# The mixer's elementwise work on GpSimd moved to VectorE and ScalarE

## The chip, the core and the metric

The kernel runs on one core of a Trainium2 chip. A core has a matrix engine (TensorE; PE in the profile, with its weight loads as PEld), VectorE (DVE), ScalarE (ACT) and GpSimd (POOL), which run side by side and wait for each other through semaphores, and queues that issue transfers between the device's memory and the on-chip memory; most of them are issued by SyncE (SP). The metric is the device time of one execution in microseconds (us), lower is better.

## The reference

One layer of a decoder, on 256 tokens of width 1024, in float32:

```python
mod = (silu(c) @ W_ada + b_ada)              # six rows of 1024: shift, scale, gate, twice
h   = rmsnorm(x) * (1 + scale1) + shift1
proj = h @ w_in                              # 1024 x 9224
y_a = stick_breaking_attention(q, k, v)      # 16 heads of 64
qk  = silu(causal_conv(proj_qk, conv_w, conv_b))   # four taps
y_b = rmsnorm(mlstm(qk, v, i, f)) * sigmoid(o)     # 4 heads of 256
x += gate1 * ((sigmoid(g_a) * (y_a @ W_a) + sigmoid(g_b) * (y_b @ W_b)) @ W_out)
h  = rmsnorm(x) * (1 + scale2) + shift2
x += gate2 * moe(h)                          # top 4 of 32 experts, clamped SwiGLU, 1024 wide
out = rmsnorm(x)
```

All up to `x += gate1 * ...` is the mixer. The experts' weights are some 400 MB, and they are read once.

## The kernel before

**Two parts.** The mixer stands first, then the experts. The experts' part multiplies the weights of one pair of experts after the other as they arrive, through a ring of slots of 1 MB each; its loads stand in order on SyncE's queue, and each waits until its slot has been read out. The last loads of the mixer and the first of the experts share these slots.

**High and low parts.** In the mixer each matrix product is taken as three products of rounded numbers: ScalarE copies a block `x` into a rounded form (the high part, `whi`, `yahi`, `ybhi`, `hhi`), and the low part is `x` minus the high part (`wlo`, `yalo`, `yblo`, `hlo`), by one `tensor_tensor` that reads two tiles on chip and writes a third. TensorE then multiplies high by high, high by low and low by high.

**The first stage** runs over eight slices `kt` of the width. `start_h(kt)` loads two rows of `W_ada`, makes the slice's scale and shift (`ada`, L169: two instructions on VectorE, each over 1024 columns of two on-chip operands, with a sum at the end), normalises the slice (L344, L346, L347), lets ScalarE round it to `hhi` (L348) and takes `hlo` (L349). `start_w(kt)` loads a slice of seven blocks of `w_in`, and in two pieces of 1024 and 768 columns ScalarE makes the high part (L332) and GpSimd the low part (L333). `start_c(kt)` issues 45 matmuls with these (L360, L363). The two buffers of high and low parts alternate between slices. L320 is the low part of the small weight of the gates.

**The attention and the mLSTM** take the other blocks of `w_in` through `chunk` (in four pieces of 512 columns: L220 the high part, L223 the low part). For the blocks named `shared` the low parts of the last two pieces stand on GpSimd, 24 in all. `conv` makes the four taps (L563, L565), ScalarE the sigmoid (L567), and GpSimd their product (L569), which the scores of the next head read. `split_b1` makes three bfloat16 parts of the experts' first bias on GpSimd (L466, L468, L469); it is used by the experts alone.

**Order.** Each engine works through its own list in order. A planner builds the lists from priorities and modelled costs; `tc.issue_after(x)` holds instructions back in the plan until `x` has been planned. `lows` collects the low parts on GpSimd, and the bias loads and some memsets on GpSimd are planned behind the last of them.

Of the kernel before, what the change touches and what calls it, by code (L numbers as in the profile page):

```python
# [18 lines left out]
AF = mybir.ActivationFunctionType  # L19
OP = mybir.AluOpType  # L20
# [43 lines left out]
def body(tc, a, out):  # L64
    nc = tc.nc
    mm = nc.tensor.matmul
    act = nc.scalar.activation
    tt = nc.vector.tensor_tensor
    ts = nc.vector.tensor_scalar
    stt = nc.vector.scalar_tensor_tensor  # L70
    f32 = lambda t: t.bitcast(F32)
# [15 lines left out]
    def next_slot(shape):  # L87

        p = slots.pop(0)
        slots.append(p)  # L90
        return p.tile(shape, F32, name=SLOT_NAME.get(p, "w"))

    def load(src, shape):
        w = next_slot(shape)
        nc.sync.dma_start(w, src)
        return w
# [59 lines left out]
    for n in range(2):  # L156
        pz = ps_z.tile([128, 2, 512], F32, name="pz")[:, 0]
        b = slice(512 * n, 512 * n + 512)
        with tc.issue_after(up):
            up = mm(pz, ones, crow[n], start=True, stop=True).ins  # L160
        s = spl.tile([128, 512], F32, name="whi")
# [44 lines left out]
        last = act(r, r, AF.Exp, scale=-0.5)  # L206
        return r, last.ins

    def chunk(src, shared=False, after=None):

        w = load(src, [128, KT, 256])
        out = []
        for qd in range(4):
            x = w[:, 2 * qd:2 * qd + 2, :]
            hi = spl.tile([128, 2, 256], F32R, name="whi")
            if after is not None and qd > 1:
                with tc.issue_after(after):
                    act(hi, x, AF.Copy)
            else:
                act(hi, x, AF.Copy)  # L220
            lo = spl.tile([128, 2, 256], F32R, name="wlo")
            eng = nc.gpsimd if shared and qd > 1 else nc.vector
            last = eng.tensor_tensor(lo, x, f32(hi), OP.subtract)  # L223
            if eng is nc.gpsimd:
                lows.append(last.ins)
            out.append((hi, lo))
        return out

    todo = []
    for c in range(2, 4):  # L230
        todo += [(a["w_in"][g], g > 3) for g in (c, 4 + c, 8 + c)[c == 2:]]
    for hd in range(4):
        todo += [(a["w_in"][g], g > 19) for g in (12 + hd, 16 + hd, 20 + hd, 24 + hd)]
    for c in range(4):
        todo += [(w, False) for w in (a["w_in"][28 + c], a["w_a"][c], a["w_in"][32 + c], a["w_b"][c])]
    todo += [(a["w_out"][c], False) for c in range(4)]
    ready = []

    def fetch(after=None):

        if todo:
            ready.append(chunk(*todo.pop(0), after))

    def take():
        if not ready:
            fetch()
        return ready.pop(0)

    def proj_T(w, mv, blocks=2):

        mhi, mlo = mv
        ps = ps_pj.tile([128, 2, T], F32, name="pj")
        for qd, (whi, wlo) in enumerate(w):
            for n in range(blocks):
                s = slice(128 * n, 128 * n + 128)
                for j in range(2):
                    kt = 2 * qd + j
                    last = kt == KT - 1
                    mm(ps[:, n, :], whi[:, j, s], mhi[:, kt, :], start=kt + n == 0, stop=False, skip_group_check=True)  # L259
                    mm(ps[:, n, :], whi[:, j, s], mlo[:, kt, :], start=False, stop=False, skip_group_check=True)  # L260
                    mm(ps[:, n, :], wlo[:, j, s], mhi[:, kt, :], start=False, stop=last, skip_group_check=True)  # L261
        return ps
# [46 lines left out]
    pif = ps_m.tile([128, 512], F32, name="pm")  # L309
    first.append(ps_m.tile([128, 512], F32, name="pm").rearrange("p (n t) -> p n t", n=2))  # L310
    wf, parts = {}, {}
    order, his, lows = [], [], []
    wi = mx.tile([128, KT, 64], F32, name="cv")
    nc.gpsimd.memset(wi, 0.0)
    nc.gpsimd.tensor_copy(wi[:, :, 0:4], wif[:, :, 0:4])
# [1 line left out]
    wihi, wilo = (mx.tile([128, KT, 64], F32R, name="cs") for _ in range(2))  # L317
    with tc.issue_after(rs1_ins):
        act(wihi, wi, AF.Copy)
    nc.gpsimd.tensor_tensor(wilo, wi, f32(wihi), OP.subtract)  # L320

    def start_w(kt):
        w = wf[kt] = next_slot([128, 1792])
        if kt:
            nc.sync.dma_start(w, a["w_first"][kt])
        else:
            for b in (slice(0, 1024), slice(1024, 1792)):
                nc.sync.dma_start(w[:, b], a["w_first"][kt][:, b])
        hi, lo = ((yahi, yalo), (ybhi, yblo))[kt % 2]
        for b in (slice(0, 1024), slice(1024, 1792)):  # L330
            x, h, l = (t[:, b] for t in (w, hi.rearrange("p a b -> p (a b)"), lo.rearrange("p a b -> p (a b)")))
            act(h, x, AF.Copy)  # L332
            lows.append(nc.gpsimd.tensor_tensor(l, x, f32(h), OP.subtract).ins)  # L333
        parts[kt] = hi, lo

    def start_h(kt):
# [28 lines left out]
    for kt in range(KT):  # L365
        if kt == KT - 1:
            start_w(kt)
            start_h(kt)
        else:
            start_h(kt)  # L370
            start_w(kt)
        start_c(kt)
# [66 lines left out]


    kp = ab.tile([128, 2, 2, T], F32, name="kp")
    with tc.issue_after(lows[-1]):
        nc.gpsimd.memset(kp[64:128, :, 0, :], 0.0)
        nc.gpsimd.memset(kp[0:64, :, 1, :], 0.0)

    qs, vs = {}, {}
    for c in range(2):
# [11 lines left out]
    def load_b1(g):  # L459
        bts[g] = mx.tile([128, 512], F32, name="bt", bufs=1)  # L460
        for i in range(4):
            nc.gpsimd.dma_start(bts[g][32 * i:32 * i + 32], a["b1"][:, 512 * g:512 * g + 512])

    def split_b1(g):
        bt, b = bts[g], b1s[:, 512 * g:512 * g + 512]
        nc.gpsimd.tensor_copy(b, bt)  # L466
        for lo in (64, 96):
            nc.gpsimd.tensor_tensor(bt[lo:128], bt[lo:128], b[lo:128], OP.subtract)  # L468
            nc.gpsimd.tensor_copy(b[lo:128], bt[lo:128])  # L469

    def step_of_b1(g):
        with tc.issue_after(lows[-1]):
            if g:
                split_b1(g - 1)
            if g < 4:
                load_b1(g)

    for c in range(4):
        if c > 2:
            qs[c] = mx.tile([128, 2, T], F32, name="q")  # L480
            pq = proj_T(take(), hT)
            fetch()
            act(qs[c], pq, AF.Copy, scale=0.125)
        q = qs[c]
        if c > 1:
            pk = proj_T(take(), hT)
            fetch()
        else:
            pk = first[1 + 4 * c]
# [10 lines left out]
        for n in range(2):  # L500
# [11 lines left out]
            l = mx.tile([128, 768], F32, name="l")  # L512
# [5 lines left out]
            hi = mx.tile([128, 768], F32R, name="so", bufs=1)  # L518
            lo = mx.tile([128, 768], F32R, name="sp")
# [3 lines left out]
            for x in (hi, lo):  # L523
                last = x is lo
# [18 lines left out]


    xpads = [ab.tile([128, 2, T + 4], F32, name=f"xpad{i}") for i in range(2)]
    with tc.issue_after(lows[-1]):
        for xp in xpads:
            nc.gpsimd.memset(xp[:, :, 0:3], 0.0)
    ve = ab.tile([128, 2, 260], F32, name="vext")
    with tc.issue_after(lows[-1]):  # L550
        nc.gpsimd.memset(ve[:, :, 256:260], 1.0)

    def conv(g, name):

        ps = proj_T(take(), hT)
        fetch()
        xp = xpads[g // 4]
        act(xp[:, :, 3:3 + T], ps, AF.Copy)
        y = mx.tile([128, 2, T], F32, name="cv")
        for n in range(2):  # L560
            ch = 2 * g + n
            tap_w = lambda j: col[:, C_CW + 4 * ch + j:C_CW + 4 * ch + j + 1]
            ts(y[:, n, :], xp[:, n, 0:T], tap_w(0), col[:, C_CB + ch:C_CB + ch + 1], op0=OP.mult, op1=OP.add)  # L563
            for j in range(1, 4):
                stt(y[:, n, :], xp[:, n, j:j + T], tap_w(j), y[:, n, :], OP.mult, OP.add)  # L565
        s = mx.tile([128, 2, T], F32, name="cs")
        act(s, y, AF.Sigmoid)  # L567
        r = mx.tile([128, 2, T], F32, name=name)
        nc.gpsimd.tensor_tensor(r, y, s, OP.mult)  # L569
        return r  # L570

    def qk_of(hd):
# [68 lines left out]
    last = None  # L641
    for hd in range(4):
# [6 lines left out]
        last = hd, read_out(hd, S), so  # L649
# [15 lines left out]
    for c in range(4):  # L665
        acc = []
        for mv in ((yahi, yalo), (ybhi, yblo)):
# [5 lines left out]
            s = mx.tile([128, 2, T], F32, name="sgate")  # L673
# [5 lines left out]
        y = acc[1]  # L679
# [26 lines left out]
    for c in range(4):  # L706
        w = take()
# [7 lines left out]
        for n in range(2):  # L715
            kt = 2 * c + n
            stt(xT[:, kt, :], po[n], mod_of(G1, kt), xT[:, kt, :], OP.mult, OP.add)
            x = xa[c // 2][:, kt % 4, :]
# [3 lines left out]
            for t in range(2):  # L722
                b = slice(128 * t, 128 * t + 128)
                mm(pl[:, 32 * t:32 * t + 32], x[:, b], rw[:, kt, :], start=False, stop=kt == KT - 1,
                   skip_group_check=True)
            for t in range(2):
                b = slice(128 * t, 128 * t + 128)
# [52 lines left out]
    def slots_of(p):  # L780

        G = wk.tile([128, 2, 2 * CAP], F32, name="G")
        for t in range(2):
            last = tt(G[:, t].rearrange("p (e s) -> p e s", e=2),
                      rank[:, t, 2 * p:2 * p + 2, None].to_broadcast([128, 2, CAP]),
                      iota[:, None, 0:CAP].to_broadcast([128, 2, CAP]), OP.is_equal)
        XG[p] = xgp.tile([128, KT, 2 * CAP], F32, name="xg")
        return G, last.ins

    XG, SS, ROWS = {}, {}, {}  # L790
    G0, last = slots_of(0)
# [299 lines left out]
    for n, (lo, width, step) in enumerate(LAST):  # L1091
        per = D // width
        for c in range(0, KT, per):
            w = next_slot([128, per, 2, width])
# [63 lines left out]
    for g in (3, 0, 1, 2):  # L1158
        b = xo[:, 2 * g:2 * g + 2, :]
        eng = nc.gpsimd if g == 3 else nc.vector  # L1160
        eng.tensor_tensor(b, b, rf[:, None, :].to_broadcast([128, 2, T]), OP.mult)  # L1161
    for g in (0, 1, 3, 2):
        eng = (nc.sync, nc.scalar)[g % 2]
# [63 lines left out]
```

## Time and profile before

| | us |
|---|---|
| median of 3 runs (lowest, highest) | 1349.43 (1348.67, 1350.36) |
| time of the profiled execution | 1350.39 |
| its span, first to last instruction | 1348.3 |
| VectorE busy | 485.9 |
| GpSimd busy | 151.3 |

The span is 2.1 us shorter than the time of the same execution. Busy time is the sum of the durations that the profiler shows, and an instruction that is held up while it runs counts as busy. The mixer takes about the first 400 us of the span.

### The profile page before, as it was taken

The numbers are of one execution on the slowest core, as the hardware profiler recorded it, in microseconds if no ns is written. First come the engines' busy times: TensorE is split into PE (matmuls) and PEld (weight loads), VectorE is DVE, ScalarE is ACT, GpSimd is POOL, SyncE is SP. The second block draws the span as 40 slices with busy tenths as digits, with TensorE's granted clock in tenths as the row PEclk, the third lists the DMA queues.
The fourth block names the chain that finished last, engine by engine and source line by source line (L and its number), as shares of the span: only waits on it lengthen the run. The fifth ranks groups of instructions, "written<-read, shape, count | busy, mean of one in ns | idle before, by whom it ended". The sixth has DMA issues, their size and how long they took to land. (4 is left out here: it accounts for less than half of the span.)

```text
span 1348.3 us, 16908 instructions
## 1 busy us (share of the span) xinstructions
PE 1239.2 (92%) x6859; PEld 675.8 (50%) x6874; DVE 485.9 (36%) x866; ACT 317.4 (24%) x600; POOL 151.3 (11%) x132
## 2 busy tenths in 40 slices
PE   7789989999998999999999999988999998899787
PEld 5777888999983443334433343332333333233323
DVE  6988888786550221121211212202121211201203
ACT  3256755655540210101101011010101101010102
POOL 5653455400000000000000000000000000000002
PEclk9899999999999999998999999999999999999989
DMA  9486465477579899999999999999999999999994
GB/s 361 150 302 226 167 255 183 168 313 283 218 278 420 364 410 421 419 419 420 421 419 420 420 420 420 421 419 420 420 421 420 419 421 420 419 420 420 419 419 163
DMA packets 70337, 483.46 MB, mean 359 GB/s; under 512 B 8134, under 2 KB 9558, under 8 KB 13676
## 3 DMA queue, kind: packets, MB, share of 16 engines
q1 hardware_dynamic: 69084, 480.54, 87.7%
q0 software_dynamic: 624, 1.23, 0.4%
q8 instruction: 57, 0.93, 0.3%
q10 hardware_dynamic: 544, 0.52, 0.1%
q14 instruction: 28, 0.23, 0.0%
HBM read 481.21 MB, written 1.05 MB: 358 GB/s over the span
## 5 line engine op out<-in xcount | busy, mean ns | idle before, releaser
L815 PE MATMUL s<-w,xg 128*64 128x512 f32 x1928 | 449.4, 602 | 29.9 <-DMA w<-in_w 26.6
L815 PEld LDWEIGHTS s<-w,xg 128*64 128x64 f32 x1928 | 125.5, 137 | 294.7 <-issue 206.8
L815 PE MATMUL t<-w,whi 128*64 128x512 f32 x908 | 204.2, 596 | 13.4 <-ACT whi L866 9.6
L832 DVE SCALAR_TENSOR_TENSOR xT<-pm,modT,xT 128x256 f32<-128x256 f32 x128 | 56.0, 479 | 392.9 <-PE pm L815 392.9
L815 PEld LDWEIGHTS t<-w,whi 128*64 128x64 f32 x908 | 61.7, 137 | 133.9 <-issue 103.7
L220 ACT ACTIVATE whi<-w 128x512 fp32r<-128x512 f32 x162 | 100.6, 630 | 85.1 <-PE pj L260 61.7
L850 ACT ACTIVATE wlo<-wlo 128x512 f32<-128x512 f32 x32 | 20.1, 630 | 424.7 <-DVE wlo L848 424.7
L223 DVE TENSOR_TENSOR wlo<-w,whi 128x512 fp32r<-128x512 f32 x140 | 101.2, 733 | 48.4 <-ACT whi L220 48.1
L261 PE MATMUL pj<-hhi,wlo 128*128 128x256 f32 x368 | 106.3, 289 | 8.8 <-DVE wlo L223 8.8
L848 DVE TENSOR_SCALAR wlo<-s 128x512 f32<-128x512 f32 x32 | 22.1, 692 | 246.2 <-PE s L815 225.1
L259 PE MATMUL pj<-hhi,whi 128*128 128x256 f32 x368 | 106.0, 288 | 0.0
L260 PE MATMUL pj<-hlo,whi 128*128 128x256 f32 x368 | 105.3, 286 | 0.0
L169 DVE CUSTOM_DVE_ANT_0 w<-w,silr,col 128x1024 f32<-128x1024 f32 x48 | 90.0, 1895 | 3.6 <-DMA w<-in_ada 3.4
L924 POOL CAST sel<-cst 128x128 bf16<-128x128 f32 x16 | 4.7, 296 | 746.2 <-PE s L815 746.2
L261 PEld LDWEIGHTS pj<-hhi,wlo 128*128 128x128 f32 x368 | 71.7, 195 | 10.2 <-DVE wlo L223 9.8
L259 PEld LDWEIGHTS pj<-hhi,whi 128*128 128x128 f32 x368 | 71.8, 195 | 0.5 <-issue 0.2
L260 PEld LDWEIGHTS pj<-hlo,whi 128*128 128x128 f32 x368 | 71.7, 195 | 0.1
L815 PEld LDWEIGHTS pm<-G,mghi 128*128 128x128 f32 x512 | 59.0, 192 | 17.6 <-issue 17.0
L815 PE MATMUL pm<-S,whi 128*128 128x256 f32 x240 | 67.3, 404 | 0.2 <-DVE xT L832 0.2
L815 PEld LDWEIGHTS pm<-S,whi 128*128 128x128 f32 x240 | 40.8, 189 | 50.0 <-issue 38.7
L815 PE MATMUL pm<-G,mghi 128*128 128x128 f32 x512 | 63.3, 279 | 0.2 <-ACT xg L843 0.2
L866 ACT ACTIVATE whi<-pm 128x512 f32<-128x512 f32 x32 | 19.1, 598 | 166.4 <-PE pm L818 166.4
(370 smaller groups left out, 1485.1 us busy)
## 6 DMA issues: line engine op xcount, KB each, us to landing
w<-in_w SPq DMA_DIRECT2D x354, 1024.0 KB, 19.9
w<-in_w_in SPq DMA_DIRECT2D x29, 1024.0 KB, 6.4
w<-in_ada SPq DMA_DIRECT2D x22, 1024.0 KB, 6.5
mglo<-in_w SPq DMA_DIRECT2D x19, 1024.0 KB, 19.9
w<-in_w_first SPq DMA_DIRECT2D x7, 896.0 KB, 14.4
w<-in_w_last SPq DMA_DIRECT2D x5, 1024.0 KB, 19.8
w<-in_w_a SPq DMA_DIRECT2D x4, 1024.0 KB, 7.0
w<-in_w_b SPq DMA_DIRECT2D x4, 1024.0 KB, 12.5
```

Source lines behind the costliest of these rows:

```text
L169: nc.vector.tensor_tensor_reduce(out=w[:, j + n, :], in0=w[:, j + n, :], in1=SILU[-1], scale=1.0, scalar=col[:, C_AB + i:C_AB + i + 1], op ...
L220: act(hi, x, AF.Copy)
L223: last = eng.tensor_tensor(lo, x, f32(hi), OP.subtract)
L259: mm(ps[:, n, :], whi[:, j, s], mhi[:, kt, :], start=kt + n == 0, stop=False, skip_group_check=True)
L260: mm(ps[:, n, :], whi[:, j, s], mlo[:, kt, :], start=False, stop=False, skip_group_check=True)
L261: mm(ps[:, n, :], wlo[:, j, s], mhi[:, kt, :], start=False, stop=last, skip_group_check=True)
L815: return tc.keep_in_program_order(mm(*args, **kw))
L832: stt(xT[:, kt, :], p[:, j, :], mod_of(G2, kt), xT[:, kt, :], OP.mult, OP.add)
L848: ts(g, glu, LIMIT, None, op0=OP.min)
L850: act(s, g, AF.Sigmoid, scale=ALPHA)
L866: act(aT[hf], pt.rearrange("p (k m) -> p k m", k=4), AF.Copy)
L924: nc.gpsimd.tensor_copy(sel, cst[:, K_EB + 2 * p:K_EB + 2 * p + 2, None].to_broadcast([128, 2, CAP]))
```

## The change

The GpSimd instructions of the mixer that work on big tiles are issued on VectorE instead: the low parts of the first stage (L333, sixteen), of the gates' weight (L320) and of the shared blocks (L223, 24), the product in `conv` (L569, eight) and the differences of the bias (L468, eight). The casts of the bias (L466, L469, twelve) are ScalarE copies. The list `lows` and what was planned behind its last entry are gone. Memsets, three small copies, the power of two columns (L621) and the selectors of the experts (L924) stay on GpSimd, as do the bias loads (L462).

```diff
-    def chunk(src, shared=False, after=None):
+    def chunk(src, after=None):
...
             lo = spl.tile([128, 2, 256], F32R, name="wlo")
-            eng = nc.gpsimd if shared and qd > 1 else nc.vector
-            last = eng.tensor_tensor(lo, x, f32(hi), OP.subtract)
-            if eng is nc.gpsimd:
-                lows.append(last.ins)
+            nc.vector.tensor_tensor(lo, x, f32(hi), OP.subtract)
...
-    nc.gpsimd.tensor_tensor(wilo, wi, f32(wihi), OP.subtract)
+    tt(wilo, wi, f32(wihi), OP.subtract)
...
             act(h, x, AF.Copy)
-            lows.append(nc.gpsimd.tensor_tensor(l, x, f32(h), OP.subtract).ins)
+            tt(l, x, f32(h), OP.subtract)
...
-    with tc.issue_after(lows[-1]):
-        nc.gpsimd.memset(kp[64:128, :, 0, :], 0.0)
-        nc.gpsimd.memset(kp[0:64, :, 1, :], 0.0)
+    nc.gpsimd.memset(kp[64:128, :, 0, :], 0.0)
+    nc.gpsimd.memset(kp[0:64, :, 1, :], 0.0)
...
-        nc.gpsimd.tensor_copy(b, bt)
+        act(b, bt, AF.Copy)
         for lo in (64, 96):
-            nc.gpsimd.tensor_tensor(bt[lo:128], bt[lo:128], b[lo:128], OP.subtract)
-            nc.gpsimd.tensor_copy(b[lo:128], bt[lo:128])
+            tt(bt[lo:128], bt[lo:128], b[lo:128], OP.subtract)
+            act(b[lo:128], bt[lo:128], AF.Copy)
 
     def step_of_b1(g):
-        with tc.issue_after(lows[-1]):
-            if g:
-                split_b1(g - 1)
-            if g < 4:
-                load_b1(g)
+        if g:
+            split_b1(g - 1)
+        if g < 4:
+            load_b1(g)
...
-        nc.gpsimd.tensor_tensor(r, y, s, OP.mult)
+        tt(r, y, s, OP.mult)
```

## Rows read from the trace of the kernel before

**Rows 1.** Busy time of each engine by stage, with clock and transfers.

```profile
core 0: us, PE busy (x) PEld busy (x) DVE busy (x) ACT busy (x) POOL busy (x), PEclk, DMA share, GB/s
0.00:84.00 84.00, 62.28 (x374) 54.06 (x375) 65.94 (x84) 24.41 (x38) 50.63 (x37) 0.92 0.70 259
84.00:160.00 76.00, 72.27 (x533) 64.17 (x531) 62.13 (x90) 54.04 (x86) 28.67 (x29) 0.98 0.66 247
160.00:290.00 130.00, 117.64 (x911) 113.50 (x910) 108.79 (x185) 74.63 (x131) 59.68 (x44) 0.97 0.54 196
290.00:400.00 110.00, 109.81 (x927) 109.19 (x926) 67.65 (x114) 54.41 (x91) 0.13 (x1) 1.00 0.72 278
...
440.00:1340.00 900.00, 841.25 (x3954) 321.25 (x3962) 171.47 (x357) 104.20 (x243) 10.05 (x19) 0.99 0.99 411
```

**Rows 2.** Who waited for whom, 10 to 90 us: total, times, longest.

```profile
ACT hhi L348 <- DVE sq L347: 45.3, 8, 6.8
...
PE pz L360 <- ACT hhi L348: 17.8, 7, 5.3
```

**Rows 3.** Timeline of VectorE in the first stage: start, duration, instruction.

```profile
12.79 1.28 DVE L169 CUSTOM_DVE_ANT_0 w<-w,silr,col 128x1024 f32<-128x1024 f32 x1
...
17.29 3.31 DVE L344 TENSOR_TENSOR sq<-xT,rs 128x256 f32<-128x256 f32 x2 [3.02 <-ACT rs L206]
20.52 0.40 DVE L347 TENSOR_SCALAR sq<-sq,A,modT 128x256 f32<-128x256 f32 x1
...
28.51 2.91 DVE L169 CUSTOM_DVE_ANT_0 w<-w,silr,col 128x1024 f32<-128x1024 f32 x1
...
31.35 3.41 DVE L169 CUSTOM_DVE_ANT_0 w<-w,silr,col 128x1024 f32<-128x1024 f32 x1
...
35.00 0.41 DVE L347 TENSOR_SCALAR sq<-sq,A,modT 128x256 f32<-128x256 f32 x1
35.90 0.43 DVE L349 TENSOR_TENSOR hlo<-sq,hhi 128x256 fp32r<-128x256 f32 x1 [0.48 <-ACT hhi L348]
...
43.19 0.41 DVE L347 TENSOR_SCALAR sq<-sq,A,modT 128x256 f32<-128x256 f32 x1
...
77.06 0.69 DVE L347 TENSOR_SCALAR sq<-sq,A,modT 128x256 f32<-128x256 f32 x1
```

**Rows 4.** Timeline of GpSimd in the same stretch.

```profile
28.49 1.85 POOL L333 TENSOR_TENSOR yblo<-w,ybhi 128x768 fp32r<-128x768 f32 x1 [3.21 <-ACT ybhi L332]
30.30 3.38 POOL L333 TENSOR_TENSOR yalo<-w,yahi 128x1024 fp32r<-128x1024 f32 x1
```

**Rows 5.** Groups of VectorE's instructions, 10 to 84 us: busy us, mean ns.

```profile
L169 DVE CUSTOM_DVE_ANT_0 w<-w,silr,col 128x1024 f32<-128x1024 f32 x16 | 42.3, 2682 | 0.0
```

**Rows 6.** The same groups, 295 to 400 us.

```profile
L223 DVE TENSOR_TENSOR wlo<-w,whi 128x512 fp32r<-128x512 f32 x64 | 44.0, 690 | 34.2 <-ACT whi L220 34.0
L169 DVE CUSTOM_DVE_ANT_0 w<-w,silr,col 128x1024 f32<-128x1024 f32 x4 | 5.1, 1279 | 0.0
```

**Rows 7.** The same groups, 84 to 160 us.

```profile
L521 DVE TENSOR_TENSOR sp<-sp,so 128x768 fp32r<-128x768 f32 x8 | 10.0, 1245 | 1.3 <-ACT so L520 1.2
```

**Rows 8.** The same groups, 160 to 290 us.

```profile
L223 DVE TENSOR_TENSOR wlo<-w,whi 128x512 fp32r<-128x512 f32 x53 | 40.3, 783 | 4.4 <-ACT whi L220 4.4
L169 DVE CUSTOM_DVE_ANT_0 w<-w,silr,col 128x1024 f32<-128x1024 f32 x14 | 24.4, 1754 | 3.6 <-DMA w<-in_ada 3.4 <-ACT silr L662 0.2
```

**Rows 9.** Groups of GpSimd's instructions over the whole span.

```profile
L223 POOL TENSOR_TENSOR wlo<-w,whi 128x512 fp32r<-128x512 f32 x24 | 42.5, 1780 | 54.0 <-ACT whi L220 17.3 <-DVE wlo L223 17.0 <-ACT l L515 12.7
...
L333 POOL TENSOR_TENSOR yblo<-w,ybhi 128x1024 fp32r<-128x1024 f32 x4 | 13.0, 3249 | 2.1 <-ACT ybhi L332 2.1
...
L468 POOL TENSOR_TENSOR bt<-bt,b1s 32x512 f32<-32x512 f32 x4 | 6.5, 1626 | 0.3
...
L569 POOL TENSOR_TENSOR v<-cv,cs 128x512 f32<-128x512 f32 x4 | 6.4, 1592 | 8.5 <-ACT cs L567 8.5
```

**Rows 10.** Who waited for whom, 160 to 295 us.

```profile
PE pj L261 <- DVE wlo L223: 8.8, 4, 3.3
```

**Rows 11.** Groups of ScalarE's instructions, 10 to 84 us.

```profile
L332 ACT ACTIVATE yahi<-w 128x1024 fp32r<-128x1024 f32 x4 | 4.2, 1048 | 1.6 <-DMA w<-in_w_first 1.6
...
L332 ACT ACTIVATE yahi<-w 128x768 fp32r<-128x768 f32 x4 | 3.3, 829 | 0.0
```

More of the change, by code (lines that the diff above doesn't have):

```diff
@@ L230, in body @@
     for c in range(2, 4):
-        todo += [(a["w_in"][g], g > 3) for g in (c, 4 + c, 8 + c)[c == 2:]]
+        todo += [a["w_in"][g] for g in (c, 4 + c, 8 + c)[c == 2:]]
     for hd in range(4):
-        todo += [(a["w_in"][g], g > 19) for g in (12 + hd, 16 + hd, 20 + hd, 24 + hd)]
+        todo += [a["w_in"][g] for g in (12 + hd, 16 + hd, 20 + hd, 24 + hd)]
     for c in range(4):
-        todo += [(w, False) for w in (a["w_in"][28 + c], a["w_a"][c], a["w_in"][32 + c], a["w_b"][c])]
-    todo += [(a["w_out"][c], False) for c in range(4)]
+        todo += [a["w_in"][28 + c], a["w_a"][c], a["w_in"][32 + c], a["w_b"][c]]
+    todo += [a["w_out"][c] for c in range(4)]
     ready = []
@@ L241, in fetch @@
         if todo:
-            ready.append(chunk(*todo.pop(0), after))
+            ready.append(chunk(todo.pop(0), after))
     def take():
@@ L311, in body @@
     wf, parts = {}, {}
-    order, his, lows = [], [], []
+    order, his = [], []
     wi = mx.tile([128, KT, 64], F32, name="cv")
@@ L545, in body @@
     xpads = [ab.tile([128, 2, T + 4], F32, name=f"xpad{i}") for i in range(2)]
-    with tc.issue_after(lows[-1]):
-        for xp in xpads:
-            nc.gpsimd.memset(xp[:, :, 0:3], 0.0)
+    for xp in xpads:
+        nc.gpsimd.memset(xp[:, :, 0:3], 0.0)
     ve = ab.tile([128, 2, 260], F32, name="vext")
-    with tc.issue_after(lows[-1]):
-        nc.gpsimd.memset(ve[:, :, 256:260], 1.0)
+    nc.gpsimd.memset(ve[:, :, 256:260], 1.0)
     def conv(g, name):
```

## The prediction

> **What bounds the kernel now.** I read the busy time by stage first. From 440 us on, TensorE is busy 841 of 900 us and the transfers run at a share of 0.99 [rows 1]: the expert weights stream, and the change touches nothing there. From 290 to 400 us TensorE is busy 109.8 of 110 us and GpSimd is idle. So whatever the change does is done in the first 290 us, and both later stretches pass it on: they begin where the mixer ends, and their loads wait for slots that the mixer's own work sets free. The transfers have room before (shares 0.54 to 0.72 [rows 1]), so an earlier mixer can also load earlier. I carry a shift of the mixer to the end one for one.
>
> In the first 84 us VectorE is busy 65.9 and GpSimd 50.6 us [rows 1]. The waits say who is late: ScalarE's `hhi` waits 45.3 us for VectorE's L347, and TensorE waits 17.8 us for that `hhi` [rows 2]. VectorE bounds this stage. Its timeline shows what fills it: from one L347 to the next (35.00 to 43.19) a slice takes 8.19 us, and most of it is two `ada` instructions of 2.91 and 3.41 us [rows 3]. The same instruction took 1.28 us at 12.79 [rows 3], and 1279 ns on average of four between 295 and 400 us, where GpSimd does nothing [rows 6]. In the slow cases GpSimd's L333 runs: it ends at 28.49 + 1.85 = 30.34, and VectorE's L169, which began at 28.51, ends at 31.42, 1.08 later; the next L333 ends at 33.68 and the next L169 at 34.76, again 1.08 later [rows 3, 4]. So VectorE's instruction lies still until GpSimd's is done. Its busy time in this stage is in good part a wait for GpSimd.
>
> Between 84 and 290 us the same is seen more weakly: L521 1245 ns for 768 columns [rows 7], L223 783 instead of 690 ns, L169 1754 instead of 1279 ns [rows 6, 8]. TensorE idles 3.7 us of the 76 and 12.4 us of the 130 [rows 1], 8.8 of them for low parts that VectorE owes [rows 10].
>
> **First stage, step by step.** What is removed from one slice's 8.19 us: 2.91 + 3.41 − 2 × 1.28 = 3.76 us of lying still [rows 3]; 4.43 us is left. What is added: a low part of 1024 and one of 768 columns. VectorE has no such instruction in the trace; the nearest are L223, 690 ns at 512 columns, and L169, 1279 ns at 1024 with two on-chip operands [rows 6]. I take 1.28 us for 1024 and halfway, 0.98, for 768. The new slice is 4.43 + 1.28 + 0.98 = 6.69 us, 1.50 less. The first and last L347 lie 77.06 − 20.52 = 56.5 us apart for seven steps [rows 3]; 7 × 6.69 = 46.8, a gain of 9.7. In front of them, two L344 take 3.31 us [rows 3]; at 256 columns one should take about 0.4 by the slope between 512 and 1024, so 2.5 us go, and the low part of 768 columns of slice 0 or the gates' low part (0.69) can stand in their place: I take 1.3 gained. Together 11.0 us.
>
> As a check, sixteen L169 lose 16 × (2682 − 1279) = 22.4 us in the stage [rows 5, 6], and the new work is 8 × (1.28 + 0.98) + 0.69 = 18.8 us; what else was held and the idle 3.02 us ahead of 17.29 [rows 3], where slice 0's low parts fit, make up the rest.
>
> Bounds. The gap of 0.48 us in front of L349 [rows 3] could take work: 7 × 0.48 = 3.4 more, so 14.4. In the other direction, ScalarE's copies in front of the two low parts take 1.05 and 0.83 us [rows 11], and if VectorE waits for a quarter of these 1.88 us, a slice takes 7.2: the stage then gains 56.5 − 7 × 7.2 + 1.3 = 7.4.
>
> The Trainium skill (Perfetto Trace Analysis, Optimizing Scalar/DVE Operations) says that work may go from a saturated VectorE to ScalarE or even GpSimd, but adds that between VectorE and GpSimd it might not help, because they share a port. By its first half this change loads the engine that bounds the stage, and the sum would be the last rival's below, 1365. By its second half, and by the same skill's SBUF — State Buffer, Who interferes with whom (a VectorE instruction with two on-chip inputs and a GpSimd one that reads on-chip memory exclude each other for a whole instruction), the durations above are lost time that comes back; the ends 1.08 us behind GpSimd's agree with this.
>
> **Attention and mLSTM, 84 to 290 us.** Added on VectorE: 24 L223, eight L468 and eight L569 [rows 9], all 512 columns, 40 × 0.69 = 27.6 us [rows 6]. Added on ScalarE: twelve bias copies, at 512 columns about 0.6 us by L332's 829 ns for 768 [rows 11], 7 us; ScalarE idles 22 and 55 us of these stages [rows 1], which hides them. Given back on VectorE: 8 × (1.245 − 0.98) = 2.1 for L521, 53 × 0.093 = 4.9 for L223, 14 × 0.475 = 6.7 for L169 [rows 6 to 8], 13.7 in all, more with the groups that I did not count. So VectorE carries up to 14 us more, and it idles 13.9 of the 76 and 21.2 of the 130 us [rows 1]: on average that hides it. If the cover is gone where it is dense, TensorE's wait for low parts grows. Against that, L569 stands between the convolution and the scores and falls from 1.59 to 0.69 us [rows 6, 9], 0.9 for each of four heads, and shared low parts come after 0.69 instead of 1.78 us. I take zero for these 206 us, between minus 12.4 (all of TensorE's idle time of the mLSTM) and plus 8 (about half of 14, through TensorE's waits).
>
> The moved instructions also stand in VectorE's list now: an L333 waits there for its high part, and what is queued behind is the next slice's L344 and `ada`; an L569 waits for the sigmoid, and the low parts behind it wait too, and TensorE for those. The bias differences wait for loads that are issued a step earlier; their price when landed is nothing beyond the 0.69 counted. The memsets that come loose on GpSimd read no tile and are costed at nothing: no row shows VectorE held by one.
>
> **Sum.** 1350.4 for the profiled execution, minus 11.0, is 1339.4. That execution was 1.0 above the median of the runs, so I forecast 1338.4.
>
> **Rivals.**
> *More than the first stage.* The conv stage recovers too: without GpSimd's holds VectorE's low parts arrive in time, and TensorE's idle 12.4 us of 160 to 290 go: 1338.4 − 12.4 = 1326; with most of it, 1329. For it: the 8.8 us wait falls on L223, 13% too long there. Against: the load that comes in is larger than the counted load that goes out.
> *The gain is given back.* VectorE is dense between 160 and 290 us (108.8 of 130), and its 14 us of new net load cost TensorE 8: 1346.
> *Slower: waits in VectorE's list.* VectorE's list puts each of the sixteen low parts right behind the ScalarE copy that feeds it, and nothing else is let past meanwhile: 8 × 1.88 = 15 us [rows 11] against 11.0 gained, 1338.4 + 15 = 1353. It decides from 11.0 / 16 = 0.69 us of waiting for each low part. Against: ScalarE idles 60 of the first 84 us [rows 1] and can copy ahead as soon as the load and the buffer are there.
> *Slower: the load is added and nothing comes back.* If the long `ada` were slow by themselves, a slice would grow by 1.28 + 0.98 = 2.26 us, seven by 15.8: 1349.4 + 15.8 = 1365. Rows 5 and 6 speak against it: the same instruction takes 1279 ns as soon as GpSimd is still.
>
> **Chances.** Forecast 0.62, with its own range 1333 to 1342; more than the first stage 0.16; given back 0.11, ending between 1342 and 1349; waits in VectorE's list 0.09; nothing comes back 0.02. A change of 0.2%, 2.7 us, is about what a measurement here can tell from none. The given-back case is faster in 0.06 and the same in 0.05. So faster 0.84, same 0.05, slower 0.11. For 8 in 10 the range reaches from 1328 to 1348: it leaves out the two slower cases, a little of the given-back one and the far end of the first.
>
> **What would show it.** In the first stage every L169 at about 1.28 us, no GpSimd work beyond memsets and copies, L333 on VectorE at 1.2 to 1.3 and about 1.0 us, L347 to L347 at 6.2 to 7.2 us, the last L347 near 66 instead of 77. Between 160 and 290 us L223 back at 0.69 us, and the stage about as long as before. From 290 us on all rows as before, shifted by about 11 us. I am wrong if L169 stays above 2 us without GpSimd, if VectorE shows idle time for L332 in front of L333, or if TensorE's wait for `wlo` grows past some 15 us.

## The result and the profile after

The changed kernel takes 1327.72 us (median of four runs, 1327.05 to 1330.19), beside 1349.09 us for the kernel before (also of four): ratio 0.9845, 95% interval 0.9831 to 0.986, 21.4 us faster. The forecast was 1338.4, faster; the time lies 0.3 us under the low end of its range. The profiled execution took 1330.19 us with a span of 1328.5. In the last experiment below one execution, of 2068.73 us at a granted clock of 0.556, is left out of the ratio.

Where the time was gained, from the starts of three instructions in the timelines:

| start of | before | after | moved |
|---|---|---|---|
| first attention queries, the end of the first stage | 81.83 | 80.85 | −1.0 |
| first branch gate, the end of attention and mLSTM | 286.05 | 265.15 | −20.9 |
| end of the span | 1348.3 | 1328.5 | −19.8 |

The first stage gained one microsecond. All the rest was gained between its end and the gates, and the experts passed it on.

Busy time by stage after the change, as in [rows 1]:

```profile
core 0: us, PE busy (x) PEld busy (x) DVE busy (x) ACT busy (x) POOL busy (x), PEclk, DMA share, GB/s
0.00:84.00 84.00, 59.00 (x390) 51.99 (x391) 58.24 (x111) 33.26 (x52) 13.39 (x35) 0.92 0.80 286
84.00:160.00 76.00, 75.52 (x571) 68.10 (x570) 66.03 (x109) 58.16 (x92) 0.00 (x0) 0.98 0.60 222
160.00:290.00 130.00, 128.10 (x1031) 125.30 (x1030) 113.41 (x227) 85.26 (x144) 4.36 (x6) 1.00 0.68 259
```

In the first 84 us VectorE is less busy than before, 58.2 instead of 65.9, with 27 more instructions: part of what it showed as work before was waiting. From 160 to 290 us (the gates now begin at 265) TensorE idles 1.9 us instead of 12.4, and its granted clock is 1.00 instead of 0.97.

The groups of VectorE, 10 to 84 us and then 160 to 290 us, answer to [rows 5] and [rows 8] (line numbers are a few lower: L330 was L333, L222 was L223):

```profile
L169 DVE CUSTOM_DVE_ANT_0 w<-w,silr,col 128x1024 f32<-128x1024 f32 x16 | 20.0, 1279 | 0.9 <-DMA w<-in_ada 0.9
L330 DVE TENSOR_TENSOR yblo<-w,ybhi 128x1024 fp32r<-128x1024 f32 x4 | 4.9, 1220 | 0.0
...
L330 DVE TENSOR_TENSOR yalo<-w,yahi 128x768 fp32r<-128x768 f32 x4 | 3.8, 952 | 0.0
...
L222 DVE TENSOR_TENSOR wlo<-w,whi 128x512 fp32r<-128x512 f32 x79 | 51.9, 685 | 5.7 <-ACT whi L220 5.4
```

All `ada` are at 1279 ns, and the moved low parts cost 1.22 and 0.95 us. So the stage should have been far shorter. VectorE's timeline, beside [rows 3], shows why it wasn't (L344 was L347, L464 is a difference of the bias):

```profile
20.74 0.69 DVE L464 TENSOR_TENSOR bt<-bt,b1s 64x512 f32<-64x512 f32 x1 [6.11 <-ACT b1s L462]
...
24.90 0.41 DVE L344 TENSOR_SCALAR sq<-sq,A,modT 128x256 f32<-128x256 f32 x1
...
50.38 0.41 DVE L344 TENSOR_SCALAR sq<-sq,A,modT 128x256 f32<-128x256 f32 x1
...
55.99 0.41 DVE L344 TENSOR_SCALAR sq<-sq,A,modT 128x256 f32<-128x256 f32 x1
...
70.57 0.41 DVE L344 TENSOR_SCALAR sq<-sq,A,modT 128x256 f32<-128x256 f32 x1
...
79.47 0.69 DVE L464 TENSOR_TENSOR bt<-bt,b1s 64x512 f32<-64x512 f32 x1 [7.07 <-ACT b1s L462]
```

A slice without bias work in VectorE's list takes 55.99 − 50.38 = 5.61 us instead of 8.19. But the first L344 starts at 24.90 instead of 20.52, and after the last slice VectorE stands still for 7.07 us. ScalarE's timeline names the cause:

```profile
20.08 0.63 ACT L462 ACTIVATE b1s<-bt 128x512 bf16<-128x512 f32 x1 [8.02 <-DMA bt<-in_b]
20.62 1.04 ACT L329 ACTIVATE yahi<-w 128x1024 fp32r<-128x1024 f32 x1
...
39.09 0.63 ACT L462 ACTIVATE b1s<-bt 128x512 bf16<-128x512 f32 x1 [5.84 <-DMA bt<-in_b]
...
78.81 0.63 ACT L462 ACTIVATE b1s<-bt 128x512 bf16<-128x512 f32 x1 [7.38 <-DMA bt<-in_b]
80.20 0.63 ACT L465 ACTIVATE b1s<-bt 64x512 bf16<-64x512 f32 x1 [0.76 <-DVE bt L464]
80.85 0.60 ACT L445 ACTIVATE q<-pz 128x512 f32<-128x512 f32 x1
```

With the ordering behind `lows` gone, the planner put the bias work into the first stage, all but the last copy. Its copies stand in ScalarE's list, and three of them wait 21 us for the bias transfer, in front of the first high part (L329) and of the queries (L445). ScalarE idles for them while the expensive chain queues behind.

### The profile page after: what moved, and what is told of

The parts are those of the page before. It is cut to its first block, busy times and chain, and to the rows that moved or that the text cites. A ratio compares the mean times of both kernels' runs of the same rounds, so it can differ in the third digit from the quotient of the medians.

```text
span 1328.5 us, 16889 instructions
## 1 busy us (share of the span) xinstructions
PE 1228.4 (92%) x6859; PEld 668.3 (50%) x6874; DVE 468.0 (35%) x923; ACT 329.9 (25%) x616; POOL 30.0 (2%) x63
## 5 line engine op out<-in xcount | busy, mean ns | idle before, releaser
L222 DVE TENSOR_TENSOR wlo<-w,whi 128x512 fp32r<-128x512 f32 x164 | 110.0, 686 | 44.3 <-ACT whi L220 43.6
L169 DVE CUSTOM_DVE_ANT_0 w<-w,silr,col 128x1024 f32<-128x1024 f32 x48 | 60.4, 1278 | 1.1 <-DMA w<-in_ada 0.9
L836 ACT ACTIVATE xg<-pm,modT 128x128 f32<-128x128 f32 x128 | 37.1, 368 | 63.5 <-PE pm L808 63.5
## 6 DMA issues: line engine op xcount, KB each, us to landing
w<-in_w SPq DMA_DIRECT2D x354, 1024.0 KB, 19.9
mglo<-in_w SPq DMA_DIRECT2D x19, 1024.0 KB, 19.9
```

The costliest lines, as they stand in the source:

```text
L169: nc.vector.tensor_tensor_reduce(out=w[:, j + n, :], in0=w[:, j + n, :], in1=SILU[-1], scale=1.0, scalar=col[:, C_AB + i:C_AB + i + 1], op ...
L222: nc.vector.tensor_tensor(lo, x, f32(hi), OP.subtract)
L836: act(xg[kt] if isinstance(xg, list) else xg[:, kt, :], p[:, width * j:width * j + width], AF.Identity, bias=mod_of(SH2, kt))
```

## The experiments

Each ratio is against the kernel before on the same chip, with its 95% interval. A hold, below, is VectorE lying still until GpSimd's instruction is done. Two theories stood against each other: A, that the first stage did get faster and lost it to the waits for the bias; and B, that the bias work leaving the middle was the gain, the first stage being bound elsewhere.

**The ordering behind the last low part, restored.**

```diff
     def step_of_b1(g):
-        if g:
-            split_b1(g - 1)
+        with tc.issue_after(lows[-1]):
+            if g:
+                split_b1(g - 1)
...
```

with `lows` filled again, now by instructions of VectorE.

> The changed kernel, with the eight bias differences and twelve bias copies on VectorE and ScalarE planned behind the last shared low part again, as before the change. Theory A (the first stage did speed up by some 10 us, and VectorE's and ScalarE's lists then lost it standing still for the bias transfers at its front and its end): the first L344 (L347 of before) starts near 19 instead of 24.9 us, the first attention queries at 70 to 73 instead of 80.9, the middle part (84 to 290 before) keeps its length within 3 us, the total falls by 8 to 11 us to about 1317 to 1320. Theory B (the middle part became shorter because the bias work left it, and the first stage is held by something else): the bias work goes back to the middle, which grows by 6 us or more, and the total is 1324 or above.

Measured: 1319.85 us, 0.9781 (0.9765 to 0.9798). Queries at 69.36, gates at 256.36: the first stage gains 11.5 more, the middle is 2.7 longer than in the changed kernel. That is A in size, but the first slice started at 27.07 where A had 19, later still: the `issue_after` acted only on the engine of the instruction it names. VectorE's differences came behind the last low part, the first of them at 88.43, but ScalarE's first copy stood ahead of the first slice and waited 10.0 us for its transfer.

**The first stage alone**, on top of the kernel before:

```diff
-            lows.append(nc.gpsimd.tensor_tensor(l, x, f32(h), OP.subtract).ins)
+            lows.append(tt(l, x, f32(h), OP.subtract).ins)
...
-    nc.gpsimd.tensor_tensor(wilo, wi, f32(wihi), OP.subtract)
+    tt(wilo, wi, f32(wihi), OP.subtract)
```

> The kernel before, with only the low parts of the first stage (L333, L320) on VectorE. Theory A: the first stage ends 9 to 14 us earlier (queries at 68 to 73 instead of 81.8 us), the middle part is as before, total 1335 to 1340. Rival (first stage bound elsewhere, by TensorE or the loads): less than 4 us.

Measured: 1330.21 us, 0.9853 (0.9836 to 0.9869), 20 us, more than the 9 to 14 that A expected. The queries start at 61.55. VectorE's timeline of this kernel:

```profile
19.26 0.41 DVE L347 TENSOR_SCALAR sq<-sq,A,modT 128x256 f32<-128x256 f32 x1
...
28.46 0.42 DVE L347 TENSOR_SCALAR sq<-sq,A,modT 128x256 f32<-128x256 f32 x1
28.79 1.22 DVE L333 TENSOR_TENSOR yalo<-w,yahi 128x1024 fp32r<-128x1024 f32 x1
29.93 0.42 DVE L349 TENSOR_TENSOR hlo<-sq,hhi 128x256 fp32r<-128x256 f32 x1
30.26 0.95 DVE L333 TENSOR_TENSOR yalo<-w,yahi 128x768 fp32r<-128x768 f32 x1
...
34.07 0.41 DVE L347 TENSOR_SCALAR sq<-sq,A,modT 128x256 f32<-128x256 f32 x1
...
58.31 0.40 DVE L347 TENSOR_SCALAR sq<-sq,A,modT 128x256 f32<-128x256 f32 x1
```

The low part of 1024 columns stands in the gap that VectorE left for ScalarE's rounding, between L347 and L349, and the next instruction begins before the shown end of the last. Seven slices take 39.05 us, 5.58 each, not 6.69.

**The middle alone**: the 24 shared low parts, the product of the convolution, and both, each on top of the kernel before.

```diff
-            eng = nc.gpsimd if shared and qd > 1 else nc.vector
-            last = eng.tensor_tensor(lo, x, f32(hi), OP.subtract)
-            if eng is nc.gpsimd:
+            last = nc.vector.tensor_tensor(lo, x, f32(hi), OP.subtract)
+            if shared and qd > 1:
                 lows.append(last.ins)
...
-        nc.gpsimd.tensor_tensor(r, y, s, OP.mult)
+        tt(r, y, s, OP.mult)
```

> The kernel before, with only the shared low parts (L223) and the product of the convolution (L569) on VectorE; first stage and bias stay on GpSimd. Theory A (these are what shortened the middle part by 20 us in the changed kernel): the first stage as before, the middle 12 to 20 us shorter, total 1329 to 1337. Theory B (the bias work that left the middle did it): the middle at most 6 us shorter, total 1343 or more.

> The kernel before, with only the 24 shared low parts (L223) on VectorE. The two moves of the middle part together gave 13.9 us. Theory A (these 24 held VectorE longest, 42.5 us of GpSimd time): 8 to 13 us gained, 1336 to 1342. Rival (the product L569, which stands between convolution and scores, was the gain): 0 to 4 us gained.

> The kernel before, with only the product of the convolution (L569) on VectorE. Theory A: 1 to 5 us gained, 1344 to 1349. Rival: 8 us or more.

Measured: both 1336.23 us, 0.9897 (0.988 to 0.9913); low parts alone 1341.18, 0.9947 (0.9931 to 0.9964); product alone 1356.32, 1.0056 (1.004 to 1.0073), slower by 7.4 us where both theories expected a gain. Together they gain 13 to 14, alone 8 and minus 7: they don't add. With both moved, queries to gates take 272.06 − 82.59 = 189.47 us, 14.8 less than before (204.22). The changed kernel takes 184.30 there, 5.2 less again, which went with the bias work: so much of B is true. The timeline of VectorE with the product alone moved shows the taps of two convolutions, and GpSimd's the work beside the first:

```profile
166.65 6.99 DVE L565 SCALAR_TENSOR_TENSOR cv<-xpad,col,cv 128x256 f32<-128x256 f32 x6
...
191.81 2.46 DVE L565 SCALAR_TENSOR_TENSOR cv<-xpad,col,cv 128x256 f32<-128x256 f32 x6
```

```profile
166.43 2.85 POOL L223 TENSOR_TENSOR wlo<-w,whi 128x512 fp32r<-128x512 f32 x2 [1.44 <-ACT whi L220]
169.22 0.80 POOL L466 CAST b1s<-bt 128x512 bf16<-128x512 f32 x1
170.10 1.21 POOL L468 TENSOR_TENSOR bt<-bt,b1s 64x512 f32<-64x512 f32 x1
171.38 0.69 POOL L469 CAST b1s<-bt 64x512 bf16<-64x512 f32 x1
172.15 1.22 POOL L468 TENSOR_TENSOR bt<-bt,b1s 32x512 f32<-32x512 f32 x1
```

Six taps take 2.46 us without GpSimd beside them and 6.99 with low parts and bias running back to back. In the kernel before, the product in GpSimd's list waited 3.26 us for ScalarE's sigmoid, and the same six taps, at 168.53, took 2.45. That this accounts for the whole 7.4 us is argued from the trace, not shown by a run of its own.

**The bias alone**, on top of the kernel before, on ScalarE and VectorE, with the loads still ordered on GpSimd:

```diff
-        nc.gpsimd.tensor_copy(b, bt)
+        act(b, bt, AF.Copy)
         for lo in (64, 96):
-            nc.gpsimd.tensor_tensor(bt[lo:128], bt[lo:128], b[lo:128], OP.subtract)
-            nc.gpsimd.tensor_copy(b[lo:128], bt[lo:128])
+            tt(bt[lo:128], bt[lo:128], b[lo:128], OP.subtract)
+            act(b[lo:128], bt[lo:128], AF.Copy)
```

> The kernel before, with only the bias work (L466 to L469) on ScalarE and VectorE, planned behind the last shared low part as before. Theory A: GpSimd's hold on VectorE of some 4 us goes, 5.5 us of new VectorE work comes: total within 3 us of before, 1346 to 1352. Theory B: 5 us or more gained, 1344 or less.

Measured: 1360.85 us, 1.0077 (1.0056 to 1.0098), 10.7 us slower. The waits, 80 to 300 us:

```profile
ACT b1s L466 <- DMA bt<-in_b: 13.5, 4, 6.1
...
PEld pz L525 <- ACT so L520: 6.3, 3, 2.8
PE pz L525 <- ACT so L520: 5.5, 3, 2.6
```

ScalarE waits 13.5 us for the bias transfer, all but 1.95 inside the attention, and TensorE behind it for the attention's rounding; the attention's last exponential starts at 170.17 instead of 159.21. B is refuted, and A, within 3 us, missed too: the bias's move by itself costs time, because its copy reaches the head of ScalarE's list before its transfer has landed.

**The bias placed late.** The changed kernel, with

```diff
         if g:
-            split_b1(g - 1)
+            with tc.issue_after(mark[0]):
+                with tc.issue_after(mark[1]):
+                    split_b1(g - 1)
```

where `mark` is the latest ScalarE and VectorE instruction of the attention or the scores, and the steps stand at columns 1 and 3 of the attention and at the first three heads. Beside it a kernel without the bias, as a bound.

> The changed kernel; each step of the bias work is queued, on ScalarE behind the latest ScalarE instruction of the attention or the scores and on VectorE behind the latest VectorE one, and the steps stand one later, so that each transfer has some 15 us or more before its copy. Theory A (the changed kernel loses some 19 us in the first stage because ScalarE's list stands still for the bias transfer, and the half hold of the first experiment left the first of these waits of 10 us and some in the attention): first L344 near 19.3 us, first queries at 61 to 63, total 1307 to 1313. Rival (what is lost in the first stage is TensorE's or the loads'): within 3 us of the first experiment, 1317 to 1322.

> The changed kernel without any bias work: the experts' first bias is left out (its tile is zero), with its loads, casts and differences. It bounds what the bias work costs in any place. Theory A: 1305 to 1311, at most 4 us below the kernel with the bias placed late. Rival: no gain over the first experiment, 1317 to 1322.

Measured: placed late 1319.0 us, 0.9786 (0.9766 to 0.9806); without bias 1310.65, 0.972 (0.9698 to 0.9742). Placed late, the first slice starts at 19.07 and the queries at 61.96, as A said: 18.9 us of the first stage had gone to the bias. The total missed A's 1307 to 1313 and lies where the rival had it, but for another reason: at the gates it is 7.1 us behind the kernel without bias (253.02 against 245.96), all of it lost in the heads of the mLSTM (the attention's last exponential starts at 133.31 in both); the 4 us allowed for that were too few. Without bias, TensorE and VectorE look like this, as in [rows 1]:

```profile
84.00:160.00 76.00, 75.36 (x593) 69.75 (x592) 65.80 (x110) 55.98 (x86) 0.00 (x0) 1.00 0.62 225
160.00:290.00 130.00, 128.74 (x1040) 126.26 (x1039) 107.89 (x212) 83.35 (x141) 4.36 (x6) 1.00 0.68 257
```

**GpSimd work that nobody waits for**, on top of the bias placed late, in the first stage on a tile that is used later:

```diff
+    flat = kp.rearrange("p a b t -> p (a b t)")
+    with tc.issue_after(wi_ins):
+        nc.gpsimd.memset(flat, 0.0)
+        for _ in range(14):
+            nc.gpsimd.tensor_tensor(flat, flat, flat, OP.mult)
```

and in its place 42 memsets of the same tile.

> The kernel with the bias placed late, plus fourteen GpSimd multiplications of a 128 x 1024 tile with itself in the first stage, which nobody waits for. Theory A (VectorE's two-input instructions lie still while GpSimd reads): L169 at 2 us and more while they run, the first stage 8 to 20 us longer than without them. Rival (the change gained because GpSimd's results came late): nobody waits for these, so L169 stays at 1.28 us and the total within 3 us.

> As the run with fourteen multiplications, but with 42 GpSimd memsets of the same tile instead, about the same GpSimd busy time and no reads. Theory A: no hold, L169 at 1.28 us, total within 3 us of the kernel with the bias placed late. Rival (any GpSimd work holds VectorE): as much longer as with the multiplications.

Measured: multiplications 1341.78 us, 0.9944 (0.9922 to 0.9966), 22.8 us longer than without; memsets 1320.62, 0.9801 (0.9779 to 0.9823), 1.6 longer. The queries start at 83.73 with the multiplications, 64.06 with the memsets, 61.96 without. VectorE's groups and GpSimd's, 10 to 84 us, with the multiplications:

```profile
L169 DVE CUSTOM_DVE_ANT_0 w<-w,silr,col 128x1024 f32<-128x1024 f32 x16 | 24.9, 1589 | 0.0
L347 DVE TENSOR_TENSOR sq<-xT,rs 128x256 f32<-128x256 f32 x8 | 8.3, 1053 | 0.0
...
L322 POOL TENSOR_TENSOR kp<-kp 128x1024 f32<-128x1024 f32 x14 | 31.2, 2226 | 1.0
```

and with the memsets:

```profile
L169 DVE CUSTOM_DVE_ANT_0 w<-w,silr,col 128x1024 f32<-128x1024 f32 x18 | 22.6, 1278 | 0.5 <-DMA w<-in_ada 0.4
L350 DVE TENSOR_SCALAR sq<-sq,A,modT 128x256 f32<-128x256 f32 x8 | 6.3, 783 | 0.2
...
L322 POOL MEMSET kp<- 128x1024 f32 x42 | 40.5, 963 | 2.2
```

31 us of GpSimd work whose results nobody needs cost 22.8 us; 40.5 us of memsets cost 2.1 at the queries. So it is the hold, not the lateness of GpSimd's results. The 1.59 us of L169 is a mean over the whole stage: the three that ran beside the multiplications (at 26.68, 31.61 and 46.08) took 2.98, 2.91 and 2.91 us, as expected, and the other thirteen 1.28. The queries came 21.8 us later, a little more than the 8 to 20 expected.

**The bias in the stage of the gates**, on ScalarE and VectorE, with marks of that stage, and there on GpSimd (the GpSimd lines of before, without the marks).

```diff
+    step_of_b1(0)
     for c in range(4):
...
+        step_of_b1(c + 1)
```

> The changed kernel with the bias work, on ScalarE and VectorE, in the stage of the branch gates, where VectorE is busy about half the time: first load ahead of it, each group's split behind one of its four columns. Theory A (the bias costs time wherever it stands in a list with no slack, and the gates have slack): within 3 us of the run without bias, 1309 to 1314. Rival (twenty instructions more cost their own 13 us of VectorE and ScalarE wherever they stand): no better than the bias in attention and scores, 1317 or above.

> The same place, but the bias work on GpSimd as before the change. Theory A: GpSimd holds VectorE's two-input instructions, so L223's mean rises in that stage, but VectorE has slack there: within 4 us of the same work on ScalarE and VectorE, 1309 to 1317. Rival (a hold costs time in any stage): 5 us or more longer.

Measured: 1312.42 us, 0.9727 (0.971 to 0.9743), and on GpSimd 1310.72, 0.9716 (0.9696 to 0.9735); the two are not told apart. Both came as A said. They beat the changed kernel by 15 to 17 us and the one before by 36 to 38. VectorE's L222 in that stage, first with the bias on ScalarE and VectorE, then on GpSimd:

```profile
L222 DVE TENSOR_TENSOR wlo<-w,whi 128x512 fp32r<-128x512 f32 x60 | 41.2, 692 | 21.2 <-ACT whi L220 20.8
```

```profile
L222 DVE TENSOR_TENSOR wlo<-w,whi 128x512 fp32r<-128x512 f32 x59 | 47.2, 814 | 17.9 <-ACT whi L220 17.8
```

GpSimd holds VectorE there too, 59 × 0.122 = 7.2 us, and it costs nothing that these runs can tell, since VectorE waits 18 us for ScalarE anyway.

## Why the prediction was right in sign and short in size

The sign was right for the reason given, the hold. The size is in part luck: the stage that was to give 11.0 us gave 1.0, and the two stages taken as zero gave 19.9.

**The hold: right, and shown.** L169 fell to 1279 ns and L223 to 685, as forecast, and the multiplications brought the hold back without anyone waiting for them. The Trainium skill (SBUF — State Buffer, Who interferes with whom) has it so, and adds that a GpSimd instruction that only writes doesn't hold one with two on-chip inputs; the memsets left L169 at 1278 ns, which agrees.

**The first stage: mis-sized, and then lost.** The term was 11.0 us. Alone, the move is worth 20.3 at the queries (81.83 to 61.55), above the upper bound of 14.4: 17.5 in the seven slices, 1.3 ahead of them, as forecast, and 1.5 behind them. The step that was off is the slice of 6.69 us; it measured 5.58. I added the durations of the low parts to a slice that had 0.48 us to spare, and counted that only as a bound of 3.4; 1.28 and 0.98 were 1.22 and 0.95; and shown durations overlap with the next instruction's by some 0.08 us. With two instructions more in a slice that is 0.7 of the 1.1 us; the rest lies in short gaps between instructions.

**The step that failed: the bias.** I costed the bias's wait at "nothing beyond the 0.69 counted" and wrote that its loads are issued a step earlier. The changed kernel has no ordering at all on that work, and the planner took it into the first stage, where ScalarE waited for the transfers. It cost 18.9 us, nearly all that the stage had gained (80.85 against 61.96). Behind the removed `issue_after` I had looked at the loads and memsets on GpSimd; the twelve copies I counted as 7 us that ScalarE's idle time hides, not as waits at the head of a list with a chain in it.

**Attention and mLSTM: taken as zero, measured 19.9 us.** The step that failed is the net load on VectorE, up to 14 us more. Here are the two stages, cut at the first queries, the attention's last exponential and the first gate, as in [rows 1]: the kernel before, the changed one, and the one with only the shared low parts and the product moved.

```profile
81.83:159.21 77.38, 73.65 (x542) 65.63 (x542) 62.72 (x90) 54.47 (x86) 28.67 (x29) 0.97 0.67 251
159.21:286.05 126.84, 114.48 (x884) 110.26 (x883) 105.99 (x182) 73.15 (x128) 59.68 (x44) 0.97 0.52 189
```

```profile
80.85:152.51 71.66, 68.89 (x510) 61.85 (x511) 61.64 (x99) 55.03 (x88) 0.00 (x0) 0.98 0.67 251
152.51:265.15 112.64, 110.74 (x886) 107.48 (x884) 98.71 (x206) 78.16 (x132) 4.36 (x6) 1.00 0.57 210
```

```profile
82.59:159.42 76.83, 71.59 (x540) 64.22 (x540) 68.10 (x98) 54.47 (x87) 30.25 (x32) 1.00 0.71 258
159.42:272.06 112.64, 110.74 (x886) 107.50 (x885) 98.76 (x206) 78.22 (x131) 4.30 (x6) 1.00 0.59 209
```

In the changed kernel VectorE is busy 160.35 us in the two stages instead of 168.71, though 24 low parts and eight products, some 22 us, came in. So some 30 us of holds went, not the 13.7 that I counted on three groups, and there was no extra load to hide.

The mLSTM is 14.2 us shorter, with the two moves alone as in the changed kernel; in neither does any bias work stand there, since GpSimd, with a shorter list, comes to all of it in the attention. TensorE idles 1.9 us of it instead of 12.4, and its own busy time fell by 3.7 us, at a granted clock of 1.00 instead of 0.97. This is the mechanism of the rival "more than the first stage", whose 12.4 was the idle time alone. That it named the time too, 1326 to 1329, is chance: it counted 11.0 us for the first stage and nothing for the attention.

The attention is 5.7 us shorter in the changed kernel, but only 0.55 with the two moves. With all the bias work on GpSimd there, L222 took 835 ns there instead of the changed kernel's 683. The kernel without bias has the changed kernel's attention (133.31 − 61.95 = 71.36 us). So the remaining 5.2 us are what the bias costs in the attention, out of which the planner took it; I had counted it as staying.

**One for one to the end: right.** −20.9 at the gates, −19.8 at the end of the span; without the bias −40.1 and −40.4. The parts add up to that: 20.3 of the first stage, 14.8 of the two moves in the middle, 5.2 of the bias leaving it: 40.3.

**Slower by waits in VectorE's list: wrong place.** The groups of L330 show at most 0.1 us of VectorE's idle time ahead of them. The mechanism exists, but on ScalarE, and for a transfer: VectorE then waits for ScalarE's copy, 6.11 and 7.07 us ahead of L464.

## What to carry to other kernels

A busy engine may be a held one: compare an instruction's duration with the same instruction where its neighbour is idle, before counting its load. GpSimd's arithmetic on on-chip tiles cost nothing that could be told where VectorE had slack (the gates), and 22.8 us for 31 us of it where VectorE bounds the stage; there a VectorE instruction, long or short, can wait for a whole one of GpSimd's. When work moves to another engine's list, carry its ordering with it: an `issue_after` is tied to an engine, and a copy that waits for a transfer stops everything that stands behind it.

## What the runs showed of the hardware that was not expected

A hold cost about the same whatever the size of the instruction held. The timeline of VectorE while GpSimd multiplied:

```profile
31.61 2.91 DVE L169 CUSTOM_DVE_ANT_0 w<-w,silr,col 128x1024 f32<-128x1024 f32 x1
...
34.45 2.10 DVE L347 TENSOR_TENSOR sq<-xT,rs 128x256 f32<-128x256 f32 x1
36.48 1.84 DVE L349 SCALAR_TENSOR_TENSOR A<-modT,col 128x1 f32<-128x1 f32 x1
```

Without GpSimd's work these take 1.28, 0.42 and 0.15 us: each is 1.6 to 1.7 us longer. Not every instruction was held: L336, 1024 columns at 40.35, took 1.21. And memsets are not wholly free: L350, a `tensor_scalar` with one on-chip tile, took 783 ns beside them instead of 412.
